# Turning the heads' outputs: TensorE transposes and one store against VectorE block transposes and stores in 128-byte pieces

## The chip, the cores and the metric

The kernel runs on one core of a Trainium2 chip. The metric is the time of one execution in device microseconds (us); the figure of a kernel is the median of its runs. Five engines work side by side, each with a queue of its own that is served strictly in order: TensorE (PE in the rows: matrix products and 128x128 transposes; PEld is its loading of weights), VectorE (DVE), ScalarE (ACT), GpSimd (POOL) and SyncE (SP), which only issues transfers (DMA). ACT and POOL issue transfers too. Engines wait for one another on semaphores.

## The reference

One decoder block over 512 rows (SEQ) of width 1024. One projection of the normalised input gives everything; the change lies in the mLSTM branch, four heads with outputs of 512 columns each:

```python
hn = rmsnorm(x, g_mix)
xa, ba, ca, za, q, k, v, o, zb, ig, fg, ga, gb = split(hn @ w_in)
ya = ((ba * causal_short_conv(ca * xa, conv_w, conv_b)) * silu(za)) @ w_a_out
hb = mlstm_chunkwise(q, k, v, ig + b_i, fg + b_f)          # 4 heads of 512 columns
hb = rmsnorm(hb, g_head)
yb = (sigmoid(o) * hb * silu(zb)) @ w_b_out
x  = x + (sigmoid(ga) * ya + sigmoid(gb) * yb) @ w_o
x  = x + sigmoid(rmsnorm(x, g_ple) @ w_ple_gate) * (p @ w_ple)
return rmsnorm(x, g_final)
```

`yb`'s product needs the heads' outputs with their columns on the partitions (the contraction runs over partitions), so what each head makes (rows on partitions) has to be turned.

## The kernel before

Every f32 product is made of three passes of fp32r products (`mm3`, L233 to L235) of a high part and a low part: ACT rounds an operand to its high part (`whi`, L180), DVE subtracts (`wlo`, L181). Weights come in chunks of 1 MB (`wraw`, four buffers) that SP loads (L148); POOL adds other chunks to them by accumulating transfers (L156), since most products run as one level of Strassen's scheme (`strassen`): seven products with about four chunks. Each product is two steps, each half of an operand is split once per step (`split_half`), and the weights' split buffers are two deep.

The order of the work is written out by hand: after each step of matmuls `step` calls `tick`, which advances every generator in `active` by one `yield`. A line of a generator between two yields thus stands in each engine's queue right behind the matmuls of that step. The order on PE, ACT, DVE and POOL is exactly the program's; SP's transfers are placed by a scheduler, and issued in its order.

Heads run one after the other. `head(h)` makes scores, the products for V and O, the weighted sum, and the gate; `y` (512 rows by 512 columns) is normed by `norm(t)` for its four row tiles t: in even heads inside a strassen run for the z gate (`sink_z`), in odd heads at once. Then `finish(h, y, wait)` waits some ticks and calls `turn`: 16 PE transposes in two groups of eight (tile `pty`), four ACT copies out of PSUM that also scale by `g_head` (`gh`, L805), and one POOL store of 1 MB into `yt_d[h]` (L813). Behind an even head runs a strassen for the merge gates (`sink_gate`), whose results `c` go through ACT's sigmoid and an ACT-issued store into `sg_d` (L782); the tag `c` has three buffers. `recut` loads the next head's q and k (`qk_d`) at that time. Behind head 3 the convolution begins (`sink_conv`), and its result tile `ya` uses the buffers of the tags `qk` and `vv`; the tile `yc` that holds the turned outputs has the tag `vv` too, of which there is one buffer.

Much later (about 628 us) POOL loads `yf[h]` from `yt_d[h]` (L1031), and `left_first` begins to make left operands of them (`left_high`, L1044 and L1045).

Of the kernel before, what the change touches and what calls it, by code (L numbers as in the profile page):

```python
# [9 lines left out]
F32 = mybir.dt.float32  # L10
F32R = mybir.dt.float32r
AF = mybir.ActivationFunctionType
ALU = mybir.AluOpType

P = 128
S = 512
NT = S // P
# [5 lines left out]
DV = 512  # L23
# [6 lines left out]
HC = 4  # L30
# [6 lines left out]
def hybrid_block(ctx, tc, x, p, g_mix, w_in, conv_w, conv_b, w_a_out, b_gates, g_head,  # L37
                 w_b_out, w_o, g_ple, w_ple_gate, w_ple, g_final, out):
    nc = tc.nc
    act, dve, pool, pe = nc.scalar, nc.vector, nc.gpsimd, nc.tensor  # L40
# [7 lines left out]
    ps_x = ctx.enter_context(tc.tile_pool(name="ps_x", bufs=4, space=bass.MemoryType.PSUM))  # L48
# [21 lines left out]
    H2 = S // 2  # L70
# [47 lines left out]
    spare = {b12[0]: None}  # L118
# [22 lines left out]
    raws, splits, pieces, active, fresh = {}, {}, deque(), [], []  # L141
# [111 lines left out]
    ident = const.tile([P, P], F32, name="ident")  # L253
# [14 lines left out]
    yt_d = [dram.tile([P, 2, HC, H2], F32, name=f"yt_d{h}") for h in range(NH)]  # L268
# [14 lines left out]
    def temp(tag, name=None, dt=F32):  # L283

        return tp.tile([P, S], dt, name=name or tag, tag=tag, bufs={"c": 3}.get(tag, 2))
# [238 lines left out]
    gh = prm[:, 40:56]  # L524
# [48 lines left out]
    def quarter(q):  # L573
        hi, lo = (u[:, q % HH, :] for u in splits[0][q // HH])
        return hi, lo, raws[0][:, q, :]
# [6 lines left out]
    hi, lo, raw = quarter(0)  # L582
# [118 lines left out]
    B = nc.vector.STREAM_SQUARE_SIZE  # L701
    rows32 = sp.tile([B, 8, S], F32, name="rows", tag="xin")
    rows = rows32[:NH]
# [92 lines left out]
        a = POFF[j] + (t - j) * P  # L796
        return u[:, a:a + P]

    def turn(h, y):

        yc = hp.tile([P, 2, 2, HC, H2], F32, name="yc", tag="vv", align_bytes=256)[:, 0]
        pts = {}
        for i in range(3):
            for v in range(2 * i - 2, 2 * i) if i else ():
                act.activation(yc[:, :, v, :], pts[v].rearrange("p (h s) -> p h s", h=2), AF.Copy,  # L805
                               scale=gh[:, 4 * h + v:4 * h + v + 1])
            for v in range(2 * i, 2 * i + 2) if i < 2 else ():
                pts[v] = ps_x.tile([P, S], F32, name="pty", tag="x")
                for t in range(NT):
                    pe.transpose(pts[v][:, t * P:(t + 1) * P], y[:, t, v * P:(v + 1) * P], ident)  # L810
            if i < 2:
                yield
        nc.gpsimd.dma_start(yt_d[h], yc)  # L813

    def qk_tile():
        both = hp.tile([P, 2, 4, S], F32R, name="qk", tag="qk", align_bytes=256)
        return [both[:, i] for i in range(2)]

    def recut(h, qk):

        for _ in range(7):
            yield
        raw = hp.tile([P, 2, 4, S], F32, name="qk_raw", tag="vv", align_bytes=256)[:, 0]
        for m in range(4):
            nc.sync.dma_start(raw[:, m, :], qk_d[h][:, m, :])
        yield
        yield
        yield
        qk.extend(qk_tile())
        for m in range(4):  # L830
            cut(qk[0][:, m, :], qk[1][:, m, :], raw[:, m, :])
            if m < 3:
                yield
# [69 lines left out]
    def head(h, qk):  # L903
        vv = []

        def sink_qk(n, t, src):

            fs, ps = slice(2 * (t % 2), 2 * (t % 2) + 2), slice(t // 2 * H2, (t // 2 + 1) * H2)
            src = src.rearrange("p (f s) -> p f s", f=2)
            if n == 1:  # L910
                nc.gpsimd.dma_start(qk_d[h + 1][:, fs, ps], src)
                return
            if not qk:
                qk.extend(qk_tile())
            cut(*[u[:, fs, ps] for u in qk], src)
            yield

        if h == 2:
            strassen(hn_lhs, sink_qk, True)
        pr = [hq2.tile([P, 1280], F32R, name=f"pr{i}", align_bytes=256) for i in range(2)]  # L920
        pp = hq2.tile([P, 1280], F32, name="pp")
        gt = []

        def sink_vo(n, t, src):
            if n == 0:
                if not vv:
                    both = hp.tile([P, 2, NT, DV], F32R, name="vv", tag="vv", align_bytes=256)
                    vv.extend(both[:, i] for i in range(2))
                act.activation(vv[0][:, t, :], src, AF.Copy)
                if t < 2:  # L930
                    yield
                dve.tensor_tensor(vv[1][:, t, :], src, vv[0][:, t, :].bitcast(F32), ALU.subtract)
            elif h % 2:
                so = temp("e", "so")
                act.activation(so, src, AF.Sigmoid)
                dve.tensor_tensor(gt[0][:, t, :], gt[0][:, t, :], so, ALU.mult)
            else:
                act.activation(gt[0][:, t, :], src, AF.Sigmoid)
            yield

        def scored():
            both = hp.tile([P, 2, NT, DV], F32, name="gty", tag="qk", align_bytes=256)
            gt.extend(both[:, i] for i in range(2))
            if h % 2:
                nc.gpsimd.dma_start(gt[0], z_d[h])

        active.append(scores(h, qk, pr, pp, scored))
        strassen(hn_lhs, sink_vo)
        gt, y = gt

        def weighted_sum(t, ps):
            dve.tensor_scalar(y[:, t, :], ps, inv[:, t:t + 1], None, ALU.mult)
            junk = temp("e", "junk")
            act.activation(junk, y[:, t, :], AF.Square, accum_out=hss[:, t:t + 1])
            yield

        for t in range(NT):
            ps = ps_x.tile([P, S], F32, name="pv", tag="x")
            for j in range(t + 1):
                mm3(ps, [ptile(u, j, t) for u in pr], [u[:, j, :] for u in vv], j == 0, j == t)  # L960
            step(weighted_sum(t, ps))

        def norm(t):
            dve.scalar_tensor_tensor(y[:, t, :], y[:, t, :], hr[:, t:t + 1], gt[:, t, :], ALU.mult, ALU.mult)

        def rsqrt():
            a, r, e = htmp
            dve.tensor_scalar(a, hss, 1.0 / DV, EPS, ALU.mult, ALU.add)
            pool.tensor_tensor(r, a, mhalf, ALU.pow)
            yield  # L970
            newton(e, a, r)
            dve.tensor_tensor(hr, r, e, ALU.mult)
            for t in range(NT) if h % 2 else ():
                norm(t)
                if t == 1:
                    yield

        def sink_z(n, t, src):
            sz = temp("e", "sz")
            act.activation(sz, src, AF.Sigmoid)  # L980
            if n == 1:
                dve.tensor_tensor(src, sz, src, ALU.mult)
                nc.gpsimd.dma_start(z_d[h + 1][:, t, :], src)
                yield
                return
            dve.tensor_tensor(sz, sz, src, ALU.mult)
            dve.tensor_tensor(gt[:, t, :], gt[:, t, :], sz, ALU.mult)
            yield
            norm(t)
            yield  # L990

        active.append(rsqrt())
        if h % 2 == 0:
            strassen(hn_lhs, sink_z)
        return y

    def finish(h, y, wait):
        for _ in range(wait):
            yield
        yield from turn(h, y)  # L1000

    hp_ctx, hp = open_pool("heads")
    hq_ctx, hq2 = open_pool("scores")
    load_maxima(0)
    qks = [qk_tile()] + [[] for _ in range(3)]
    for h in range(NH):
        y = head(h, qks[h])
        active.append(finish(h, y, 2 + h % 2))
        if h % 2 == 0:
            active.append(recut(h + 1, qks[h + 1]))  # L1010
            strassen(hn_lhs, sink_gate(h))
    close(hq_ctx)

# [15 lines left out]
    yf = {h: (wbp if h == 3 else yfp).tile([P, 2, HC, H2], F32, name=f"yf{h}", tag=f"yf{h}", align_bytes=256) for h in (0, 2, 1, 3)}  # L1029
# [6 lines left out]
    def left_high(k):  # L1036
# [7 lines left out]
        act.activation(units[k][0], src, AF.Copy, scale=scale)  # L1044
        return lambda: dve.scalar_tensor_tensor(both[:, 1], src, scale, both[:, 0].bitcast(F32), ALU.mult, ALU.subtract)  # L1045

    def left_first():
        for _ in range(5):
            yield
        for k in range(3):  # L1050
            low = left_high(k)
            yield
            low()
            yield
        for g in range(2):
            (a11, a21), (a12, a22) = ([yf[2 * g + r][:, v] for v in range(2)] for r in range(2))
            dve.tensor_tensor(hsf[g], a22, a21, ALU.subtract)
            yield
            dve.tensor_tensor(a21, a11, a21, ALU.subtract)
            yield  # L1060
            dve.tensor_tensor(a11, hsf[g], a11, ALU.add)
            yield
            if g == 0:
                dve.tensor_tensor(a12, a11, a12, ALU.subtract)
                yield
# [337 lines left out]
    q = [slice(CW, CW + CW // 2), slice(CW + CW // 2, D)]  # L1403
# [50 lines left out]
```

## Time and profile before

| what | us |
| --- | --- |
| median of 3 runs (lowest, highest) | 845.53 (845.3, 846.86) |
| the profiled execution | 847.37 |
| its span, as the trace has it | 845.6 |
| PE busy | 834.5 |
| DVE, ACT, POOL busy | 651.0, 495.5, 210.0 |
| granted TensorE clock, mean | 0.998 |

In the timelines a row is: start in us from the span's start, duration, engine, line, operation, out<-in tiles, shape, count, and in brackets how long the engine was idle before it and what ended that. `PEld` rows are weight loads. Rows with a q (SPq, ACTq) are the issue of a transfer.

### The profile page before, as it was taken

The page shows a single profiled execution, that of the slowest core. Times are in us where ns is not written, and L with a number is a line of the kernel's source. Part 1 is how long each engine was busy: PE and PEld are TensorE (multiplying, and loading weights), DVE is VectorE, ACT ScalarE, POOL GpSimd, SP SyncE. Part 2 cuts the span into 40 slices and gives each one's busy share as a digit, 9 for nine tenths or more (in the row PEclk, how much of TensorE's full clock was granted, in tenths as well). Part 3 has the DMA queues.
Part 4 walks back from the last instruction along what each step waited for, and adds up shares of the span by engine and source line. Part 5 has one row for each costly group of instructions (what it writes and reads, how often), then busy time and mean ns, then how long its engine had stood idle before and what let it go on. Part 6 is the DMA issues. An engine that isn't in the chain of part 4 may idle for free.

```text
span 845.6 us, 12113 instructions
## 1 busy us (share of the span) xinstructions
PE 834.5 (99%) x4584; PEld 726.7 (86%) x4584; DVE 651.0 (77%) x878; ACT 495.5 (59%) x720; POOL 210.0 (25%) x203
## 2 busy tenths in 40 slices
PE   8999999999999999999999999999999999999996
PEld 7888888887889988888788999999998888888885
DVE  5788767975787677788668779897986677999565
ACT  6467665666865566665776654555453256667543
POOL 5203122203124321220222333433411122131031
PEclk9999999999999999999999999999999999999999
DMA  9748779779978997896898799899989488999402
GB/s 310 269 145 183 159 166 220 194 274 227 252 159 207 244 225 180 199 215 199 258 243 211 156 218 169 194 184 182 181 255 380 101 194 214 284 258 229 187 0 100
DMA packets 103939, 173.89 MB, mean 206 GB/s; under 512 B 5632, under 2 KB 46132, under 8 KB 102600
## 3 DMA queue, kind: packets, MB, share of 16 engines
q0 software_dynamic: 39488, 70.33, 44.6%
q1 hardware_dynamic: 59792, 94.64, 33.7%
q10 hardware_dynamic: 4600, 8.14, 3.1%
q8 instruction: 36, 0.59, 0.3%
q14 instruction: 23, 0.19, 0.1%
HBM read 156.30 MB, written 16.79 MB: 205 GB/s over the span
## 4 chain that ended last, share of the span: by engine, by line
PE 92%; DMA 3%; DVE 2%; issue 1%; ACT 1%; SPq 0%; POOL 0%; POOLq 0%; ACTq 0%; DVEq 0%
PE mm L234 28%; PE mm L235 28%; PE mm L233 28%; PE pv L233 1%; PE pv L235 1%; PE pv L234 1%; DMA wraw<-in_w_ple 1%; DMA wraw<-in_w_b_out 1%; PE pty L810 1%; DMA sg_d<-c 1%; PE sc L235 1%; PE sc L234 1%; PE sc L233 1%; DVE wlo L181 1%; PE ptk L1247 0%
## 5 line engine op out<-in xcount | busy, mean ns | idle before, releaser
L181 DVE TENSOR_TENSOR wlo<-wraw,whi 128x1024 fp32r<-128x1024 f32 x244 | 299.4, 1229 | 104.7 <-ACT whi L180 98.8
L180 ACT ACTIVATE whi<-wraw 128x1024 fp32r<-128x1024 f32 x246 | 257.1, 1054 | 103.8 <-PE mm L235 48.8
L156 POOL DMA_DIRECT2D wraw<-in_w_in x112 | 136.9, 1423 | 335.4 <-DVE wlo L181 207.7
L346 ACT ACTIVATE s<-mm 128x512 f32<-128x512 f32 x84 | 50.2, 597 | 100.2 <-PE mm L235 98.7
L233 PE MATMUL mm<-whi,hs 128*128 128x512 f32 x256 | 99.9, 390 | 0.0
L234 PE MATMUL mm<-wlo,hs 128*128 128x512 f32 x256 | 99.8, 390 | 0.0
L235 PE MATMUL mm<-whi,hs 128*128 128x512 f32 x256 | 99.7, 389 | 0.0
L233 PE MATMUL mm<-hn_hi,whi 128*128 128x256 f32 (+1 forms) x304 | 93.3, 307 | 0.0
L235 PE MATMUL mm<-hn_hi,wlo 128*128 128x256 f32 (+1 forms) x304 | 92.9, 306 | 0.0
L234 PE MATMUL mm<-hn_lo,whi 128*128 128x256 f32 (+1 forms) x304 | 92.8, 305 | 0.0
L233 PE MATMUL mm<-hs,whi 128*128 128x256 f32 x320 | 90.9, 284 | 0.0
L234 PE MATMUL mm<-hs,whi 128*128 128x256 f32 x320 | 90.5, 283 | 0.0
L235 PE MATMUL mm<-hs,wlo 128*128 128x256 f32 x320 | 90.5, 283 | 0.0
L234 PE MATMUL mm<-wlo,hn_hi 128*128 128x512 f32 x192 | 75.3, 392 | 0.4 <-DVE wlo L181 0.2
L233 PE MATMUL mm<-whi,hn_hi 128*128 128x512 f32 x192 | 74.9, 390 | 0.0
L235 PE MATMUL mm<-whi,hn_lo 128*128 128x512 f32 x192 | 74.8, 389 | 0.0
L234 PEld LDWEIGHTS mm<-hs,whi 128*128 128x128 f32 x320 | 61.4, 192 | 0.0
L233 PEld LDWEIGHTS mm<-hs,whi 128*128 128x128 f32 x320 | 61.4, 192 | 0.0
L235 PEld LDWEIGHTS mm<-hs,wlo 128*128 128x128 f32 x320 | 61.4, 192 | 0.0
L235 PEld LDWEIGHTS mm<-hn_hi,wlo 128*128 128x128 f32 x304 | 58.1, 191 | 2.5
L234 PEld LDWEIGHTS mm<-hn_lo,whi 128*128 128x128 f32 x304 | 58.1, 191 | 2.4
L233 PEld LDWEIGHTS mm<-hn_hi,whi 128*128 128x128 f32 x304 | 58.1, 191 | 2.4
(339 smaller groups left out, 1670.2 us busy)
## 6 DMA issues: line engine op xcount, KB each, us to landing
wraw<-in_w_in SPq DMA_DIRECT2D x32, 1024.0 KB, 6.1
wraw<-in_w_in POOLq DMA_DIRECT2D x52, 512.0 KB, 8.5
wraw<-in_w_in SPq DMA_DIRECT2D x48, 512.0 KB, 5.6
wraw<-in_w_in POOLq DMA_DIRECT2D x60, 256.0 KB, 5.7
wraw<-in_w_b_out SPq DMA_DIRECT2D x7, 1024.0 KB, 7.0
wraw<-in_w_b_out POOLq DMA_DIRECT2D x12, 512.0 KB, 7.0
wraw<-in_w_o SPq DMA_DIRECT2D x5, 1024.0 KB, 7.4
yt_d<-yc POOLq DMA_DIRECT2D x4, 1024.0 KB, 4.9
```

The lines of the kernel that those rows point to most:

```text
L156: nc.gpsimd.dma_start(raws[to][:, ks, cs], src[:, ks, :], accum_op=ALU.add)
L180: act.activation(hi, t, AF.Copy)
L181: (e_lo or dve).tensor_tensor(lo, t, hi.bitcast(F32), ALU.subtract)
L233: pe.matmul(ps, lhsT=a[0], rhs=b[0], start=first, stop=False, **kw)
L234: pe.matmul(ps, lhsT=a[0], rhs=b[1], start=False, stop=False, **kw)
L235: pe.matmul(ps, lhsT=a[1], rhs=b[0], start=False, stop=last, **kw)
L346: act.activation(to[i], src, AF.Copy, scale=scale)
L810: pe.transpose(pts[v][:, t * P:(t + 1) * P], y[:, t, v * P:(v + 1) * P], ident)
```

## The change

The 64 PE transposes, the 16 ACT copies behind them and the four 1 MB stores go. Instead DVE transposes each row tile of `y` (128x512) in blocks of 32x32 (one instruction a tile, `turn`), into the first half of a `vv` buffer. That leaves the blocks themselves in the wrong places; the store places them: `put(i, b)` issues four transfers on SP, each from 32 partitions with 8x32 contiguous pieces of 32 elements, that is 256 pieces of 128 bytes. A head has eight puts, 32 transfers. `recut` uses the second half of the same buffer (`spare`) instead of a tile of its own. In even heads tiles 0 and 1 are turned inside the z strassen and put during the first four ticks behind the head, tiles 2 and 3 are turned four ticks later and put over four ticks more. In odd heads the tiles are turned from the fifth tick on and put over four ticks behind that; the first two cuts of q and k of head 2 come four ticks later than before. The scaling by `g_head` is done by 16 ACT instructions on the loaded `yf` in `left_first` (`scale_head`), in a loop that is one tick longer.

```diff
@@ -796,31 +796,55 @@
         a = POFF[j] + (t - j) * P
         return u[:, a:a + P]
 
-    def turn(h, y):
-
-        yc = hp.tile([P, 2, 2, HC, H2], F32, name="yc", tag="vv", align_bytes=256)[:, 0]
-        pts = {}
-        for i in range(3):
-            for v in range(2 * i - 2, 2 * i) if i else ():
-                act.activation(yc[:, :, v, :], pts[v].rearrange("p (h s) -> p h s", h=2), AF.Copy,
-                               scale=gh[:, 4 * h + v:4 * h + v + 1])
-            for v in range(2 * i, 2 * i + 2) if i < 2 else ():
-                pts[v] = ps_x.tile([P, S], F32, name="pty", tag="x")
-                for t in range(NT):
-                    pe.transpose(pts[v][:, t * P:(t + 1) * P], y[:, t, v * P:(v + 1) * P], ident)
-            if i < 2:
-                yield
-        nc.gpsimd.dma_start(yt_d[h], yc)
+    def turning(h):
+
+        both = hp.tile([P, 2, NT, DV], F32, name="yc", tag="vv", align_bytes=256)
+        blocks, spare = (both[:, i] for i in range(2))
+        blocks = blocks.rearrange("p t v -> p (t v)").rearrange("p (i v t c) -> p i v t c", i=2, v=HC, c=P)
+        to = yt_d[h].rearrange("p i v (t b a) -> p i (v t) b a", b=P // B, a=B)
+
+        def turn(y, t):
+            dve.transpose(blocks[:, t // 2, :, t % 2, :], y[:, t, :])
+
+        def put(i, b):
+            rows = blocks[b * B:(b + 1) * B, i].rearrange("p v t (q a) -> p (v t) q a", a=B)
+            for q in range(P // B):
+                nc.sync.dma_start(to[q * B:(q + 1) * B, i, :, b, :], rows[:, :, q, :])
+
+        return turn, put, spare
+
+    def finish(h, y, tools):
+
+        turn, put, _ = tools or turning(h)
+        if h % 2:
+            for ts in ((),) * 4 + (((0,), (1,), (2,), (3,)) if h == 1 else ((0, 1), (), (2,), (3,))):
+                for t in ts:
+                    turn(y, t)
+                yield
+            for b in range(P // B):
+                for i in range(2):
+                    put(i, b)
+                yield
+            return
+        for i in range(2):
+            for b in range(P // B):
+                put(i, b)
+                yield
+            if i == 0:
+                for _ in range(4):
+                    yield
+                for t in (2, 3):
+                    turn(y, t)
+                    yield
 
     def qk_tile():
         both = hp.tile([P, 2, 4, S], F32R, name="qk", tag="qk", align_bytes=256)
         return [both[:, i] for i in range(2)]
 
-    def recut(h, qk):
+    def recut(h, raw, qk):
 
         for _ in range(7):
             yield
-        raw = hp.tile([P, 2, 4, S], F32, name="qk_raw", tag="vv", align_bytes=256)[:, 0]
         for m in range(4):
             nc.sync.dma_start(raw[:, m, :], qk_d[h][:, m, :])
         yield
@@ -910,6 +934,8 @@
             if n == 1:
                 nc.gpsimd.dma_start(qk_d[h + 1][:, fs, ps], src)
                 return
+            for _ in range(4 if t < 2 else 0):
+                yield
             if not qk:
                 qk.extend(qk_tile())
             cut(*[u[:, fs, ps] for u in qk], src)
@@ -988,26 +1014,28 @@
             yield
             norm(t)
             yield
-
+            if t < 2:
+                yield
+                if not tools:
+                    tools.extend(turning(h))
+                tools[0](y, t)
+                yield
+
+        tools = []
         active.append(rsqrt())
         if h % 2 == 0:
             strassen(hn_lhs, sink_z)
-        return y
-
-    def finish(h, y, wait):
-        for _ in range(wait):
-            yield
-        yield from turn(h, y)
+        return y, tools
 
     hp_ctx, hp = open_pool("heads")
     hq_ctx, hq2 = open_pool("scores")
     load_maxima(0)
     qks = [qk_tile()] + [[] for _ in range(3)]
     for h in range(NH):
-        y = head(h, qks[h])
-        active.append(finish(h, y, 2 + h % 2))
+        y, tools = head(h, qks[h])
+        active.append(finish(h, y, tools))
         if h % 2 == 0:
-            active.append(recut(h + 1, qks[h + 1]))
+            active.append(recut(h + 1, tools[2], qks[h + 1]))
             strassen(hn_lhs, sink_gate(h))
     close(hq_ctx)
 
@@ -1044,14 +1072,23 @@
         act.activation(units[k][0], src, AF.Copy, scale=scale)
         return lambda: dve.scalar_tensor_tensor(both[:, 1], src, scale, both[:, 0].bitcast(F32), ALU.mult, ALU.subtract)
 
+    def scale_head(h):
+        for v in range(HC):
+            act.activation(yf[h][:, :, v, :], yf[h][:, :, v, :], AF.Copy, scale=gh[:, HC * h + v:HC * h + v + 1])
+
     def left_first():
         for _ in range(5):
             yield
+        for h in (0, 2):
+            scale_head(h)
+            yield
         for k in range(3):
             low = left_high(k)
             yield
             low()
-            yield
+            if k:
+                scale_head(2 * k - 1)
+                yield
         for g in range(2):
             (a11, a21), (a12, a22) = ([yf[2 * g + r][:, v] for v in range(2)] for r in range(2))
             dve.tensor_tensor(hsf[g], a22, a21, ALU.subtract)
```

On SP, between the loads of weights around the end of head 0 (wrawN is the N-th chunk of weights, qk_d1 the stored q and k of head 1, yt_d0 the turned output of head 0), stood before:

```order
L148 DMA wraw14_1277<-in_w_in 128x4x512
L148 DMA wraw15_1357<-in_w_in 128x4x512
L148 DMA wraw16_1403<-in_w_in 128x4x512
L825 DMA qk_raw_1651<-qk_d1_94 128x512
L148 DMA wraw17_1609<-in_w_in 128x4x512
L825 DMA qk_raw_1651<-qk_d1_94 128x512 x3
L148 DMA wraw18_1649<-in_w_in 128x4x512
L148 DMA wraw19_1692<-in_w_in 128x4x512
L148 DMA wraw20_1739<-in_w_in 128x4x512
```

and now:

```order
L148 DMA wraw14_1277<-in_w_in 128x4x512
L812 DMA yt_d0_90<-yc_1321 32x8x32 x5
L148 DMA wraw15_1360<-in_w_in 128x4x512
L812 DMA yt_d0_90<-yc_1321 32x8x32 x3
L148 DMA wraw16_1406<-in_w_in 128x4x512
L812 DMA yt_d0_90<-yc_1321 32x8x32 x8
L148 DMA wraw17_1602<-in_w_in 128x4x512
L148 DMA wraw18_1642<-in_w_in 128x4x512
L148 DMA wraw19_1685<-in_w_in 128x4x512
L812 DMA yt_d0_90<-yc_1321 32x8x32 x4
L148 DMA wraw20_1737<-in_w_in 128x4x512
L812 DMA yt_d0_90<-yc_1321 32x8x32 x12
```

Sixteen of the 32 transfers stand ahead of chunk 17, four ahead of chunk 20 and twelve behind it; the loads of q and k have moved ahead of chunk 13.

On DVE the turns of head 0's tiles 2 and 3 (`STREAM_TRANSPOSE yc<-gty`, L807) stand one behind each of the two splits of the 24th operand (`wlo240`, `wlo241`), each ahead of a result `c` of the gate strassen.

The second place is ACT, in the gate strassen behind head 0, where it issues the stores of the results (L782; whi261 is the high half of the 26th operand, L240 a cut of the next head's q and k). The semaphores waited for stand in brackets; DMAHW0 to DMAHW7 are the eight that all transfers of SP and ACT share. Before:

```order
L781 ACTIVATE c_1733<-c_1733 128x512 [waits DVE_49]
L782 DMA sg_d1_97<-c_1733 128x512 [waits Activation_49]
L781 ACTIVATE sg_1782<-mm_1459 128x512 [waits PE_49]
L782 DMA sg_d0_96<-sg_1782 128x512 [waits Activation_49]
L180 ACTIVATE whi261_1785<-wraw17_1609 128x1024
L240 ACTIVATE qk_1714<-qk_raw_1651 128x512 [waits DMAHW7_49]
L781 ACTIVATE c_1759<-c_1759 128x512 [waits DMAHW2_49,DVE_49]
L782 DMA sg_d1_97<-c_1759 128x512 [waits Activation_49]
```

and now:

```order
L781 ACTIVATE c_1731<-c_1731 128x512 [waits DMAHW6_49,DVE_49]
L782 DMA sg_d1_97<-c_1731 128x512 [waits DMAHW1_49,Activation_49]
L781 ACTIVATE sg_1788<-mm_1462 128x512 [waits PE_49]
L782 DMA sg_d0_96<-sg_1788 128x512 [waits DMAHW4_49,Activation_49]
L180 ACTIVATE whi261_1791<-wraw17_1602 128x1024
L240 ACTIVATE qk_1712<-yc_1321 128x512
L781 ACTIVATE c_1761<-c_1761 128x512 [waits DMAHW2_49,DVE_49]
L782 DMA sg_d1_97<-c_1761 128x512 [waits DMAHW1_49,Activation_49]
```

The rows are the same ones; what is new is that each store's issue waits for the transfer that used its semaphore last (a put, a load of SP or an earlier store), with the ACT rows behind it.

The third place is DVE at the beginning of the convolution, behind head 3 (cv and m are its intermediate tiles, ya1 its first result in the buffer that held the turned outputs). It stands now:

```order
L181 TENSOR_TENSOR wlo760_4787<-wraw46_4445,whi760_4786 128x1024 [waits DMAHW5_49,DMAHW4_49,Activation_49]
L410 TENSOR_TENSOR ya1_4754<-cv_4235,ya0_4753 128x2x256 [waits DMAHW4_49,DMAHW5_49,DMAHW3_49,DMAHW6_49,DMAHW2_49,DMAHW7_49,DMAHW1_49,DMAHW0_49]
L447 TENSOR_TENSOR m_4230<-m_4230,cz_4756 128x512
L181 TENSOR_TENSOR wlo761_4820<-wraw46_4445,whi761_4819 128x1024 [waits Activation_49]
L399 TENSOR_SCALAR cv_4235<-cu_4234,prm_174 128x256 [waits DVE_49]
```

Before, the L410 row waited for one semaphore, that of POOL's one store of head 3. Now it waits for all eight, that is for the last of head 3's 32 puts, and the split wlo761 stands two rows behind it. On SP these puts stand 3 behind chunk 45, 9 behind chunk 46, 12 behind chunk 47 and 8 behind chunk 48.

## The prediction

> **What bounds the kernel now.** I read the page's engine shares first, then busy times by stretch, then the chain of waits. The page's busy times:
>
> ```profile
> PE 834.5 (99%) x4584; PEld 726.7 (86%) x4584; DVE 651.0 (77%) x878; ACT 495.5 (59%) x720; POOL 210.0 (25%) x203
> ```
>
> PE is busy for 834.5 of a span of 845.6 us. The stretches tell where it isn't:
>
> ```profile
> core 0: us, PE busy (x) PEld busy (x) DVE busy (x) ACT busy (x) POOL busy (x), PEclk, DMA share, GB/s
> 20.00:195.00 175.00, 175.00 (x798) 145.47 (x797) 135.78 (x179) 110.42 (x166) 33.02 (x31) 1.00 0.76 203
> 195.00:200.00 5.00, 4.92 (x21) 3.46 (x20) 4.09 (x5) 3.79 (x6) 2.43 (x3) 1.00 0.87 283
> 200.00:404.00 204.00, 204.00 (x1088) 176.66 (x1087) 150.70 (x203) 126.13 (x189) 52.95 (x50) 1.00 0.88 211
> 404.00:418.00 14.00, 13.67 (x60) 10.67 (x59) 9.65 (x12) 11.23 (x18) 1.57 (x2) 1.00 0.83 268
> 418.00:820.00 402.00, 401.80 (x2452) 361.14 (x2451) 325.90 (x420) 223.20 (x306) 107.40 (x95) 1.00 0.84 204
> ```
>
> From 20 to 820 us PE stands still for 0.6 us in all (0.08 behind head 0, 0.33 behind head 2, 0.20 later), at a granted clock of 1.00. All heads lie there, so PE's work is the time, and whatever makes PE wait is added to it whole. The two small holes, at 195 and 404 us, lie behind the even heads, where the change acts, and there the transfers are at 0.87 and 0.83 of their engines' time: that is where a loss would start.
>
> **What is removed.** The chain of waits holds the transposes as eight rows, two for each head, each of eight transposes; the first and the last:
>
> ```profile
> 164.90 0.87 PE pty L810 x8
> ...
> 480.24 0.87 PE pty L810 x8
> ```
>
> Eight times 0.87 is 7.0 us of PE on the chain: the gain. What they feed (ACT copies, a store of 1 MB) isn't on the chain.
>
> **DVE turns.** 16 instructions of 128x512. The trace has four of that operation, and these gaps of DVE, near the ends of heads:
>
> ```profile
> L891 DVE STREAM_TRANSPOSE pp<-pp 128x512 f32<-128x512 f32 x4 | 2.8, 706 | 0.0
> 143.80 0.69 DVE L350 TENSOR_TENSOR c<-s,mm 128x512 f32<-128x512 f32 x1 [1.88 <-ACT s L346]
> 183.67 0.69 DVE L350 TENSOR_TENSOR c<-s,mm 128x512 f32<-128x512 f32 x1 [1.20 <-ACT s L346]
> 263.19 0.69 DVE L241 TENSOR_TENSOR qk<-c,qk 128x512 fp32r<-128x512 f32 x1 [1.93 <-ACT qk L240]
> 481.85 1.23 DVE L181 TENSOR_TENSOR wlo<-wraw,whi 128x1024 fp32r<-128x1024 f32 x1 [1.97 <-ACT whi L180]
> ```
>
> At 706 ns that is 11.3 us of DVE in all, 0.71 at a time, one in each tick but at head 3. DVE stands idle for 1.2 to 1.97 us before the next result or split, so the turns cost nothing. If that cover were gone, each turn would hold up the next split by 0.71, at most 11.3 in all.
>
> **ACT.** 16 copies go and 16 scalings of 128x512 come, late:
>
> ```profile
> L805 ACT ACTIVATE yc<-pty,prm x16: 672/682/692, 166.5 to 482.3; 128x512 f32<-128x512 f32 x16
> 640.00:656.00 16.00, 16.00 (x73) 13.23 (x72) 11.14 (x12) 5.22 (x6) 0.00 (x0) 1.00 0.96 368
> ```
>
> By 682 ns they are 10.9 us, in a stretch where ACT is busy for 5.2 of 16 us and PE never waits. They just fit; if the loads of `yf` come a tick later, the first left operands do too. I take 0 (bounds 0 to 3, less than a tick of 3.5, which is the distance of two gate stores below).
>
> **SP.** 32 issues a head, each with an issue time as in these rows (three in 1.62, two in 0.92):
>
> ```profile
> 176.64 1.62 SPq L825 DMA_DIRECT2D qk_raw<-qk_d  x3
> 501.25 0.92 SPq L148 DMA_DIRECT2D wraw<-in_w_in  x2
> ```
>
> At 0.5 us a head's puts hold SP for 16 us, over 8 to 12 ticks, that is about 2 us in a tick of 3.5. Weight loads behind them in SP's queue start up to 4 us later (eight puts between two chunks). Four buffers keep those loads more than one use ahead, so I take 0, and let the price of a piece carry what the DMA engines lose.
>
> **A piece of 128 bytes.** No row before has one. The 16 DMA engines' time by packets (packets, MB, share), for the whole run and in two windows (500 to 580 and 186 to 204 us), is nearest:
>
> ```profile
> q1 hardware_dynamic: 59792, 94.64, 33.7%
> ...
> q1 hardware_dynamic: 8367, 8.31, 33.8%
> ...
> q1 hardware_dynamic: 1113, 2.20, 38.4%
> ```
>
> A packet took 76 ns at 1583 bytes (0.337 x 845.6 x 16 / 59792), 51.7 ns at 993 and 99.4 ns at 1977. A line through pairs of these comes to 10 to 16 ns at 128 bytes; I take p = 13 ns. Below lies 6 ns (128/993 of 51.7), above 52 ns, if small packets cost as much as the smallest mean seen. A put is 256 pieces, 16 for each engine.
>
> [...]
>
> **Gate stores behind the even heads.** Around the hole at 195 us:
>
> ```profile
> 194.93 0.69 DVE L350 TENSOR_TENSOR c<-s,v 128x512 f32<-128x512 f32 x1 [2.77 <-DMA sg_d<-c]
> 195.54 1.22 DVE L181 TENSOR_TENSOR wlo<-wraw,whi 128x1024 fp32r<-128x1024 f32 x1
> 196.81 0.19 PEld L234 LDWEIGHTS mm<-wlo,hn_hi 128*128 128x128 f32 x1 [0.40 <-DVE wlo L181]
> ...
> 194.35 0.33 ACTq L782 DMA_DIRECT2D sg_d<-c  x1
> 197.85 0.33 ACTq L782 DMA_DIRECT2D sg_d<-c  x1
> ...
> sg_d<-c ACTq DMA_DIRECT2D x4, 256.0 KB, 3.9
> ```
>
> DVE waits 2.77 us for a store of `c` to free its buffer, the split queued behind it follows, and PE waits 0.40 for the split: no slack. The store takes 3.9 us; in that time one tick's four puts share its engines, 64 pieces on each, 64p = 0.83. Twice (heads 0 and 2): 128p = 1.66 us. The new semaphore waits of ACT's issues: the store at 197.85 waits for the one of 194.35, which lands at 194.35 + 3.9 = 198.25, so 0.4 late, with a sigmoid and a weight rounding behind it on ACT, and DVE's split behind that. I take 0, as that split is a step ahead; bounds 0 and 2.
>
> **Weights behind them.** The twelve puts behind chunk 20 (three ticks, about 10 us) run beside the accumulating transfers that the next splits wait for (head 0, then head 2):
>
> ```profile
> 208.39 1.06 ACT L180 ACTIVATE whi<-wraw 128x1024 fp32r<-128x1024 f32 x1 [2.47 <-DMA wraw<-in_w_in]
> 209.48 1.23 DVE L181 TENSOR_TENSOR wlo<-wraw,whi 128x1024 fp32r<-128x1024 f32 x1 [1.71 <-ACT whi L180]
> 210.76 0.19 PEld L234 LDWEIGHTS mm<-wlo,hs 128*128 128x128 f32 x1
> ...
> 426.27 1.06 ACT L180 ACTIVATE whi<-wraw 128x1024 fp32r<-128x1024 f32 x1 [1.62 <-DMA wraw<-in_w_in]
> 427.36 1.23 DVE L181 TENSOR_TENSOR wlo<-wraw,whi 128x1024 fp32r<-128x1024 f32 x1 [0.86 <-ACT whi L180]
> 429.60 0.19 PEld L234 LDWEIGHTS mm<-wlo,hs 128*128 128x128 f32 x1
> ```
>
> ACT waits 2.47 us for the transfer; the split ends at 210.71 and PE uses it at 210.76. Half of the twelve puts fall into that transfer's time, 96p = 1.25 us late, all of it PE's. At head 2 the split ends at 428.59, 1.0 ahead of its use: 96p - 1.0 = 0.25. Together 1.5.
>
> **The convolution's first write.**
>
> ```profile
> 509.51 0.68 DVE L410 TENSOR_TENSOR ya<-cv,ya 128x512 fp32r<-128x512 f32 x1
> 511.58 1.23 DVE L181 TENSOR_TENSOR wlo<-wraw,whi 128x1024 fp32r<-128x1024 f32 x1 [0.78 <-ACT whi L180]
> 513.82 0.19 PEld L235 LDWEIGHTS mm<-hn_hi,wlo 128*128 128x128 f32 x1
> ...
> wraw<-in_w_in SPq DMA_DIRECT2D x16, 512.0 KB, 4.4
> ...
> yt_d<-yc POOLq DMA_DIRECT2D x4, 1024.0 KB, 4.9
> ```
>
> The store of 1 MB took 4.9 us and was long done here. Now L410 waits for the last of 32 puts, eight of them behind chunk 48, whose pair is issued from 501.25 and lands 4.4 later. Eight issues at 0.5, a put in flight and some waiting for semaphores bring it to about 511.5 (estimate from these rows), 2 us later than L410 stands now. Behind it on DVE stand `m` and the split of 511.58, whose end at 512.81 is 1.0 ahead of its use; with 0.78 idle ahead of it too, 2.0 late leaves nothing to 1.2; I take 0.8 (bounds 0 to 3).
>
> **Sum.** -7.0 + 1.66 + 1.25 + 0.25 + 0.8 = -3.04. The profiled execution's 847.37 would become 844.3. It stands 1.84 above the median of 845.53; on the median it is 842.5. In p the sum is 320p - 7.2.
>
> **Rivals.** *All hidden:* the puts run in the gaps of the transfers and nothing waits: 845.53 - 7.0 = 838.5. The share of 0.76 in the first stretch speaks for it, 0.87 behind head 0 against it. This stands for p of 6 ns or less as well (320p - 7.2 = -5.3, 840.2).
>
> *Given back whole:* p between 17 and 28 ns puts the sum between -1.7 and +1.7. [...] The same outcome has a second way: the transfers of weights are the bound behind the even heads, PE comes there 1.74 us earlier twice and only waits longer, so 3.5 of the gain goes and -3.0 becomes +0.5: 846.0. The wait of 2.47 us for a transfer speaks for it; against it, those transfers are started by work that PE paces, so that they come earlier too. [...]
>
> *Slower:* small pieces cost a fixed time each. From 22.5 ns on the change loses; at 28 ns it is +1.7, at 42 ns +6.2 (851.8), at 52 ns +9.4 (855). The place is the gate stores and the weights behind heads 0 and 2, with no slack in the rows above. Against it speaks the fall from 99 to 52 ns when a packet halves, which leaves little that is fixed.
>
> *The change doesn't do what it says:* the transposes go from PE in any case; only where PE would wait in their place is open, and that is the second way above.
>
> **How the numbers follow.** Less than 0.2%, 1.7 us, can't be told from no change. Chances: all hidden (838.5 to 840.2) 0.22; part given back (p of 6 to 17 ns, 840.2 to 843.8, its own range) 0.34; given back whole (843.8 to 847.2) 0.20; slower (847.2 to 855) 0.24. So faster 0.56, same 0.20, slower 0.24. The likeliest is the second case, with 842.5 from the sum. The range leaves out the upper part of the slower case, from p = 42 ns on, some 0.1, and little below all hidden: 838.3 to 852.
>
> **What the profile after would show.** Right: no `pty`, PE busy about 7 us less; 16 transposes on DVE of 0.7 us with no split waiting behind them; packets of q1 32,768 more, and their share grown by p of 13 ns each (0.4 ms over 16 engines, 3% of the span); holes of PE of 1 to 3 us only near 195 to 210, 404 to 430 and 511 to 515 us. Wrong: a share of q1 grown by more than 6% (p over 25 ns), or stores of `sg_d` of 6 us; PE waiting at ends of odd heads; SP late with weights; or PE holes at 640 to 660 behind the scalings.

## The result, and the profile after

The changed kernel takes 867.07 us (866.33 to 868.26, 4 runs) against 845.65: a ratio of 1.0252, 95% interval 1.0234 to 1.027. It is 21.4 us slower; the prediction was 842.5 with a range of 838.3 to 852. The page of the changed kernel, and the same stretches of time as before (its span is 865.3 us, so each lies up to 20 us earlier in the program):

```profile
PE 837.0 (97%) x4520; PEld 724.0 (84%) x4520; DVE 659.5 (76%) x894; ACT 495.3 (57%) x720; POOL 207.8 (24%) x199
...
core 0: us, PE busy (x) PEld busy (x) DVE busy (x) ACT busy (x) POOL busy (x), PEclk, DMA share, GB/s
20.00:195.00 175.00, 174.46 (x784) 143.90 (x782) 139.96 (x184) 108.23 (x162) 33.16 (x31) 1.00 0.77 201
195.00:200.00 5.00, 5.00 (x23) 3.86 (x22) 1.83 (x2) 2.01 (x3) 2.85 (x4) 1.00 1.13 275
200.00:404.00 204.00, 197.25 (x1015) 168.57 (x1014) 147.14 (x203) 119.87 (x179) 50.68 (x46) 0.97 0.89 201
404.00:418.00 14.00, 14.00 (x64) 11.59 (x63) 12.36 (x14) 7.83 (x12) 0.00 (x0) 1.00 0.77 243
418.00:820.00 402.00, 390.96 (x2380) 350.20 (x2379) 317.89 (x409) 226.24 (x310) 100.87 (x90) 0.99 0.87 210
```

PE has 64 instructions fewer and is yet busy for 2.5 us longer. Between 200 and 820 us it stands still for 17.8 us, where it was 0.5 before, and in two stretches the granted clock is below 1. What PE waits for:

```profile
PE mm L233 <- ACT v L346: 7.1, 2, 4.7
PE mm L235 <- DVE wlo L181: 6.0, 1, 6.0
PE mm L234 <- DVE wlo L181: 3.4, 6, 1.0
```

Two waits of ACT and one of DVE make 13.1 us. What those engines waited for stands in the view of the tile `yc` (the turned blocks): who waited for transfers of it, in us and times, and how long those took to land:

```profile
  ACT vv L955: 16.8, 3
  DVE ya L410: 7.7, 1
...
DMA to landing us min/median/max: 1.7/5.5/16.8
```

These are waits for puts (a put, from here on, is one of the transfers of 256 pieces). The view also puts 6.5 us of POOL down to a put, but in the kernel before POOL is idle for 6.49 us at the same place, so that is no loss. The timelines show the four large waits, three of them with PE's row behind the hole (the first held PE up by 0.1 us itself):

```profile
218.21 0.63 ACT L955 ACTIVATE vv<-c 128x512 fp32r<-128x512 f32 x1 [4.72 <-DMA yt_d<-yc]
...
313.04 0.63 ACT L955 ACTIVATE vv<-c 128x512 fp32r<-128x512 f32 x1 [6.77 <-DMA yt_d<-yc]
314.21 0.80 PE L233 MATMUL mm<-whi,hs 128*128 128x512 f32 x1 [4.66 <-ACT v L346]
...
446.09 0.63 ACT L955 ACTIVATE vv<-c 128x512 fp32r<-128x512 f32 x1 [5.27 <-DMA yt_d<-yc]
447.26 0.50 PE L233 MATMUL mm<-whi,hs 128*128 128x512 f32 x1 [2.44 <-ACT v L346]
...
529.32 0.69 DVE L410 TENSOR_TENSOR ya<-cv,ya 128x512 fp32r<-128x512 f32 x1 [7.70 <-DMA yt_d<-yc]
531.80 0.58 PE L235 MATMUL mm<-hn_hi,wlo 128*128 128x256 f32 x1 [6.03 <-DVE wlo L181]
```

`vv` is the next head's V. It lies in the one buffer of its tag, which the turned blocks held until the last put had landed. On SP, eight puts behind head 1 take 10.87 us to be issued, with a load of weights behind them:

```profile
290.60 10.87 SPq L812 DMA_DIRECT2D yt_d<-yc  x8
301.57 4.70 SPq L148 DMA_DIRECT2D wraw<-in_w_in  x1
```

Where the time goes, by the start of the same matrix product in the two traces (after minus before, in us):

| matmul at (before) | delay | what lies between |
| --- | --- | --- |
| 158.2 | +0.2 | head 0 up to its end |
| 169.1 | -1.4 | two groups of transposes gone |
| 204.8 | +2.3 | holes of 0.81 and 0.76, then a slow clock |
| 218.2 | +3.4 | weights late, and ACT's first wait for `vv` |
| 262.3 | +1.7 | two groups gone |
| 310.6 | +9.1 | the hole of 4.66, then a slow clock |
| 387.7 | +7.9 | two groups gone |
| 437.1 | +12.4 | small holes at 430, the hole of 2.44 |
| 454.2 | +13.6 | a hole of 0.99 behind POOL's load of `gty` |
| 480.9 | +12.1 | two groups gone |
| 515.3 | +19.7 | the hole of 6.03, then a slow clock |
| the end | +19.8 | |

### The profile page after: what moved, and what is told of

Its sections match the earlier page's. It is cut to its first block, busy times and chain, and to the rows that moved or that the text cites. A ratio compares the mean times of both kernels' runs of the same rounds, so it can differ in the third digit from the quotient of the medians.

```text
span 865.3 us, 12151 instructions
## 1 busy us (share of the span) xinstructions
PE 837.0 (97%) x4520; PEld 724.0 (84%) x4520; DVE 659.5 (76%) x894; ACT 495.3 (57%) x720; POOL 207.8 (24%) x199
## 4 chain that ended last, share of the span: by engine, by line
PE 75%; DMA 12%; DVE 5%; ACT 3%; SPq 3%; issue 2%; ACTq 0%; POOL 0%; POOLq 0%; DVEq 0%
PE mm L234 23%; PE mm L235 23%; PE mm L233 23%; DMA yt_d<-yc 7%; DMA wraw<-in_w_in 2%; SPq L812 2%; DVE wlo L181 2%; ACT whi L180 1%; PE pv L235 1%; PE pv L234 1%; PE pv L233 1%; DMA wraw<-in_w_b_out 1%; DMA xin<-in_x 1%; DMA z_d<-c 0%; PE ptk L1284 0%
## 5 line engine op out<-in xcount | busy, mean ns | idle before, releaser
L156 POOL DMA_DIRECT2D wraw<-in_w_in x112 | 137.1, 1448 | 387.7 <-DVE wlo L181 204.4
L233 PE MATMUL mm<-whi,hs 128*128 128x512 f32 x256 | 101.3, 396 | 7.5 <-ACT v L346 7.1
L235 PE MATMUL mm<-whi,hs 128*128 128x512 f32 x256 | 100.7, 393 | 0.0
L233 PEld LDWEIGHTS mm<-whi,hs 128*128 128x128 f32 x256 | 48.6, 190 | 18.9 <-ACT v L346 7.8
```

Source lines behind the costliest of these rows:

```text
L156: nc.gpsimd.dma_start(raws[to][:, ks, cs], src[:, ks, :], accum_op=ALU.add)
L233: pe.matmul(ps, lhsT=a[0], rhs=b[0], start=first, stop=False, **kw)
L235: pe.matmul(ps, lhsT=a[1], rhs=b[0], start=False, stop=last, **kw)
```

## The experiments

The kernel before took 846.0 to 846.3 us beside these runs.

**One store in place of the puts.**

```diff
 def put(i, b):
-    rows = ...
-    for q in range(P // B):
-        nc.sync.dma_start(...)
+    if i == 1 and b == P // B - 1:
+        nc.gpsimd.dma_start(yt_d[h], <the blocks as they lie>)
```

> Leaves out the placing: the turned blocks of a head go to DRAM as they lie, by one POOL store of 1 MB where the last put stood (the blocks stay in the wrong places). The turns on DVE and the late scaling on ACT stay. Three theories of the loss. Turns: the DMA engines take packets of different queues in turn, so each of a put's 16 small packets on an engine waits for a 2048-byte packet of POOL's accumulating transfers (median 176 ns), 2.9 us a put, and the late puts hold buffers that ACT and DVE wait for. Price: the 128-byte pieces take engine time (15 ns, 31 us over 16 engines) and weights come late for it. Issue: 128 more issues on SP and the eight shared semaphores hold up SP's weight loads. All three: 838.5, within 838 to 840, PE without new holes. If it stays over 845, the turns on DVE or the scaling cost what was thrown on the puts.

846.81 us, ratio 1.0002 (0.9991 to 1.0013). All three theories missed: the large holes are gone, but the gain isn't kept. The start of products stood 3.8 us ahead of before at head 2's end (417 to 441 us) and 0.9 behind it at 454 us, by three holes of 0.68 to 0.76 us and 3.4 us at half the clock (mean granted clock 0.995, before 0.998). The store stands in the burst of accumulating transfers behind the even heads; behind head 0 the chain of waits runs through these:

```profile
196.79 8.35 DMA wraw<-in_w_in
207.85 13.95 DMA wraw<-in_w_in
```

The second one, the same transfer as the one issued at 211.01 in the kernel before, took 10.54 there. So 1 MB in that burst costs time in one plain store too.

**The same transfers in pieces of 1 KB.**

```diff
-    rows = blocks[b * B:(b + 1) * B, i].rearrange("p v t (q a) -> p (v t) q a", a=B)
+    rows = blocks[b * B:(b + 1) * B, i].rearrange("p v t c -> p v (t c)")
     for q in range(P // B):
-        nc.sync.dma_start(to[q * B:(q + 1) * B, i, :, b, :], rows[:, :, q, :])
+        nc.sync.dma_start(yt_d[h][b * B:(b + 1) * B, i, q], rows[:, q])
```

> The same 128 SP transfers in the same places with the same bytes, each in 32 pieces of 1 KB in place of 256 of 128 bytes (so the blocks land in wrong places). Turns: two packets an engine and put, some 0.4 us beside accumulating transfers; the holes at 309, 445 and 526 us go, 838.5 to 843. Price: 46 ns for 1 KB, 11.8 us of engine time in place of 31, so about 0.38 of the loss of 28 us stays: 849. Issue: the number of issues and semaphores is the same, so nothing changes: 864 to 868.

850.86 us, ratio 1.0043 (1.0026 to 1.006): 16.2 of the 21.4 us go with the number of pieces alone, at the same bytes, issues and places. That refutes the theory of issues as the main cause, but the time lies nearest to what the theory of price gave (849), not to the theory of turns (838.5 to 843), so this run doesn't tell those two apart. PE no longer waits for `vv`, and behind `ya` for 0.3 us only; the longest hole that is left, 2.15 us, stands behind this:

```profile
203.50 0.33 ACTq L782 DMA_DIRECT2D sg_d<-sg  x1
203.87 1.06 ACT L180 ACTIVATE whi<-wraw 128x1024 fp32r<-128x1024 f32 x1 [1.74 <-DMA yt_d<-yc]
```

ACT's issue of a gate store waits for a put with the same semaphore, and the rounding of weights behind it is late: this part is what the theory of issues says. The other holes, 6.8 us in all between 150 and 730 us, were not traced to a cause.

**Puts issued by POOL.**

```diff
-                nc.sync.dma_start(to[q * B:(q + 1) * B, i, :, b, :], rows[:, :, q, :])
+                nc.gpsimd.dma_start(to[q * B:(q + 1) * B, i, :, b, :], rows[:, :, q, :])
```

> The same 128-byte pieces, issued by POOL in the same places. Turns: the puts stand in the same queue as the accumulating transfers and no longer share the engines with them packet by packet, each takes 0.2 to 0.5 us when its turn comes, but POOL needs 0.6 to 1.2 us for each issue, which delays accumulating transfers: 842 to 852. Price: the pieces cost the same: 862 to 868. Issue: SP is free of the puts: 840 to 848, with SP's weight loads as before the change.

861.55 us, ratio 1.0164 (1.0138 to 1.019): near the theory of price, but not for its reason. Within a group the puts land 0.2 to 0.6 us apart (in the median 3.9 us from issue to landing, 5.5 in the changed kernel), SP is free of them (which by the theory of issues gave 840 to 848), and the holes have moved: 4.69 us at 285, where DVE waits 8.84 for a store of `qk_d` that stands behind 24 puts in POOL's queue, and 4.65 at 514, where `ya` still waits for the last put:

```profile
287.66 0.69 DVE L350 TENSOR_TENSOR c<-s,v 128x512 f32<-128x512 f32 x1 [8.84 <-DMA qk_d<-c]
...
516.19 0.69 DVE L410 TENSOR_TENSOR ya<-cv,ya 128x512 fp32r<-128x512 f32 x1 [6.31 <-DMA yt_d<-yc]
```

**Other buffers, puts on SP as in the changed kernel.** The second half of a head's blocks gets a buffer of its own, head 3's lie in the tile `m`, and in odd heads the first half's puts go ahead of the second's.

```diff
-        both = hp.tile([P, 2, NT, DV], F32, name="yc", tag="vv", align_bytes=256)
+        if h < 3:
+            both = hp.tile([P, 2, NT, DV], F32, name="yc", tag="vv", align_bytes=256)
+            halves = [<the first 4 KB of both>, hp.tile([P, 2 * DV], F32, name="yd", tag="yd", align_bytes=256)]
+        else:
+            halves = [m[:, i] for i in range(2)]
...
-            for b in range(P // B):
-                for i in range(2):
-                    put(i, b)
+            for k in range(0, 8, 2):
+                for n in (k, k + 1):
+                    put(n // 4, n % 4)
```

> Output as in the reference. The second half of a head's turned blocks gets a buffer of its own (4 KB), so that only the first half's puts hold the buffer that the next head's vv needs; head 3's blocks lie in the unused half of the merge tile m, so that the convolution's ya does not wait for puts. In odd heads the first half's eight put groups come ahead of the second's. Turns: puts stay slow (2.6 us apart beside accumulating transfers), but PE's holes of 4.66, 2.44 and 6.03 us and the slower clock behind them (2.6 and 1.5 us) go: 847 to 853. Price: weights stay late, only the wait for the buffers goes: 855 to 864. Issue: SP's queue is as long as before: 858 to 866.

847.05 us, ratio 1.0008 (0.9986 to 1.003), the low end of what the theory of turns gave, and 8 us below the theory of price. The puts are as slow as in the changed kernel (2.6 to 3.1 us apart behind head 0) and cost the same engine time; q1 in the changed kernel, then here:

```profile
q1 hardware_dynamic: 94608, 98.85, 36.8%
...
q1 hardware_dynamic: 94608, 98.85, 38.0%
```

Yet 20 us are gone, of the 28.4 that lie between the changed kernel and the gain that was due. So the theory of price is out, and most of the loss was the wait for two buffers, with what followed from it. (Some 1.6 of the 20 are luck: the holes of 1.14 and 0.75 us behind head 0 bring no half clock here, with a mean granted clock of 0.997, see below.) What is left is a load on SP that lands 16 us after its issue beside puts, and a gate store that takes 6.5 us, for which the next gate store's issue waits, as the chain of waits shows at 290 and 193 us:

```profile
290.60 16.07 DMA wraw<-in_w_in
...
193.60 6.50 DMA sg_d<-c
```

**The removal alone.**

```diff
-        yc = hp.tile(...)
-        <16 transposes, four copies>
-        nc.gpsimd.dma_start(yt_d[h], yc)
+        yield
+        yield
+        nc.gpsimd.dma_start(yt_d[h].rearrange("p i v s -> p (i v s)"), y.rearrange("p t s -> p (t s)"))
```

> The kernel before without the 64 PE transposes and the 16 ACT copies; POOL's 1 MB store stands at the same place and stores the heads' outputs unturned and unscaled. It tells what the removal is worth by itself. If PE's 7.0 us come out whole: 838.5, within 838 to 840. If the weights' transfers behind heads 0 and 2 are the bound there, PE only waits longer: 3.5 us of it stay, 842.

848.82 us, ratio 1.0027 (1.0016 to 1.0038): slower, against both forecasts, by a wait that the edit itself made. The store now reads `y`, and behind head 1 ACT waits for it to free the buffer of the tag `qk`:

```profile
266.16 0.63 ACT L240 ACTIVATE qk<-c 128x512 fp32r<-128x512 f32 x1 [10.06 <-DMA yt_d<-gty]
```

PE stands still for 5.73 us there. Everywhere else the products come earlier by 0.8 to 0.9 us behind each group that is gone, and keep it through the bursts. The wait and the half clock behind it (mean granted clock 0.993) cost 7.9 us by the products' starts, and the last product is 0.6 late, so without them it would be some 7.2 early (an estimate). The removal is worth what was forecast, and a transfer that holds a buffer can take it back.

**Plain stores in quiet places.** The buffers of the run before last, but each half goes out in one POOL store of 512 KB, in even heads the second one behind the burst.

```diff
+            if b == q == 0:
+                nc.gpsimd.dma_start(yt_d[h][:, i].rearrange("p v s -> p (v s)"), halves[i].rearrange("p v t c -> p (v t c)"))
```

> The turns on DVE, the late scaling and the buffers of the run named buffers, but each head's turned blocks go out as they lie, in two POOL stores of 512 KB, the second behind the gate products' accumulating transfers in even heads. It leaves out the placing. If turns and scaling are hidden and the loss of the run with one store came from where that store stood (in the burst of accumulating transfers behind heads 0 and 2), this is as fast as the removal by itself: 838 to 841. If the turns on DVE delay splits: 844 to 848, with PE waiting for DVE behind the turns.

841.72 us, ratio 0.9941 (0.9921 to 0.996). Its page:

```profile
PE 827.4 (99%) x4520; PEld 720.3 (86%) x4520; DVE 660.8 (79%) x894; ACT 495.6 (59%) x720; POOL 212.1 (25%) x207
```

In the profiled executions PE is busy for 7.1 us less than before and the last product comes 6.5 earlier; by the medians the gain is 4.3, with four runs. No hole stands behind the turns on DVE or the late scaling.

**Puts on POOL, in quiet places, with the new buffers.**

```diff
-                nc.sync.dma_start(...)
+                nc.gpsimd.dma_start(...)
+        yield from puts(0, 4)          # even heads: first half, four transfers a tick
+        ...                            # turn the second half, then eight ticks behind the burst
+        yield from puts(1, 2)
+            yield from puts(0, 4 if h == 1 else 1)
+            for _ in range(6 if h == 1 else 0):
+                yield
+            yield from puts(1, 2 if h == 1 else 1)
```

> Output as in the reference. The 128-byte puts are issued by POOL, so that they stand in line with the accumulating transfers and not against them; the buffers are those of the run named buffers; the first half of a head is put four transfers a tick where POOL has no accumulating transfers, the second half two a tick (head 3 one a tick) behind the burst. Turns: no put is in an engine's queue beside a burst, no buffer is waited for, ACT's stores share no semaphore with a put: 838.5 to 842. Price: the pieces still take 31 us of engine time, weights late as in the changed kernel: 855 to 865. Issue: 128 issues of 0.58 us on POOL delay accumulating transfers: 844 to 850.

845.77 us, ratio 1.0003 (0.9977 to 1.003), scattered from 840.28 upwards: unclear by itself. Its one large hole is 4.17 us at 233, behind this row:

```profile
234.82 0.69 DVE L976 TENSOR_TENSOR gty<-gty,so 128x512 f32<-128x512 f32 x1 [5.25 <-DMA gty<-z_d]
```

The load of `gty` stands behind ten puts and two accumulating transfers on POOL.

**The same, with that load ahead of the puts.**

```diff
-        for _ in range(8):
+        for _ in range(13):
             yield
-        yield from puts(1, 2)
+        yield from puts(1, 4)
-            for _ in range(6 if h == 1 else 0):
+            for _ in range(10 if h == 1 else 0):
```

> Output as in the reference. As the run named poolbuf, with the second half's puts moved behind POOL's load of gty (even heads, four a tick) and behind the last accumulating transfer of the first gate products (head 1), since in poolbuf DVE waited 5.25 us for that load behind four puts. Turns: no hole at 233 us; 840 to 842, the time of the run named halves (841.7), clear of the kernel before. Price: the pieces' engine time stays, so no better than poolbuf, 845 to 850. Issue: POOL's 128 issues delay the accumulating transfers of the next products: 845 to 850, with holes at 245 to 270 us.

841.37 us, ratio 0.9941 (0.992 to 0.9962): faster than both kernels, with the same placing in pieces of 128 bytes as the changed kernel, and level with the plain stores. Its page and packets, then the packets of the changed kernel:

```profile
PE 828.3 (99%) x4520; PEld 720.0 (86%) x4520; DVE 660.0 (78%) x894; ACT 496.1 (59%) x720; POOL 282.8 (34%) x327
...
DMA packets 107459, 173.89 MB, mean 207 GB/s; under 512 B 7616, under 2 KB 48116, under 8 KB 106632
q0 software_dynamic: 43008, 70.34, 45.6%
...
DMA packets 138180, 173.89 MB, mean 201 GB/s; under 512 B 40385, under 2 KB 80885, under 8 KB 137353
q0 software_dynamic: 38912, 66.14, 41.7%
```

POOL's 128 issues (75 us more of its time than in the changed kernel) are hidden. But the small packets are gone as well. Issued by SP, each piece of 128 bytes is a packet of its own, 32,768 in all. Issued by POOL, the 4.2 MB of puts that q0 has more than in the changed kernel are 2048 packets of 2 KB (the other 2048 packets that it has more are under 512 B): 16 for each put, one for 16 of its 256 pieces. So POOL's queue packed the pieces here, in the first run with puts on POOL too (q0 there: 43008 packets, 70.34 MB as well), and these runs say nothing on what single pieces cost. No run separates the packing from the other ticks.

## Why the prediction was wrong, by its steps

**The gain of 7.0 us, the turns and the scaling** were right. The products' starts move by 0.9 us at nearly every group, and these rows have no wait behind them; their instructions took

```profile
L807 DVE STREAM_TRANSPOSE yc<-gty 128x512 f32<-128x512 f32 x16 | 11.1, 700 | 0.0
L1077 ACT ACTIVATE yf<-yf,prm 128x512 f32<-128x512 f32 x16 | 10.1, 708 | 0.0
```

against 706 and 682 ns in the sum.

**The price of a piece**, 13 ns, was right as engine time where little else ran, with some luck: two of the three pairs of points in the prediction give 10 and 16 ns, the third, of 1583 and 1977 bytes, gives less than nothing. In the whole run q1 has 34,816 packets more and, by its share, 15.4 ns for each (0.368 x 865.3 less 0.337 x 845.6, times 16). Between 286 and 290 us, where almost nothing else ran, it is 12.2 ns (0.315 x 4.0 x 16 / 1652), and in the burst, from 204 to 210 us, 25.7 ns (0.112 x 6.0 x 16 / 418). The two windows:

```profile
q1 hardware_dynamic: 1652, 0.20, 31.5%
q0 software_dynamic: 37, 0.08, 21.5%
...
q0 software_dynamic: 459, 0.89, 80.2%
...
q1 hardware_dynamic: 418, 0.05, 11.2%
```

**The step that failed first is "64p = 0.83"**: a put's delay was taken to be the sum of its pieces' own times. In the burst q0 (POOL's accumulating transfers, 1.9 KB a packet) and q1 (the puts) had almost the same number of packets served, 459 and 418, but 0.89 and 0.05 MB. The counts fit engines that turn from one queue to the other packet for packet, so that each of the 16 pieces that an engine has of a put (256 over 16 engines) waits for a packet of 168 ns (0.802 x 6.0 x 16 / 459). By this estimate a put takes 2.7 us, where 0.2 was counted, and four puts in a row behind head 0 landed 2.6 to 2.7 us apart (208.27, 210.88, 213.56, 216.17). The run with 1 KB pieces, two packets on each engine, took 16 us of the loss away. What a packet is depended on the queue in these runs, one piece of 128 bytes where SP issued the puts and 16 pieces, 2 KB, where POOL did; the two counts, nearly level, are of such packets.

**The step that was left out is the buffer.** The sum has a term for `ya` (0.8, bounds 0 to 3; measured 6.03) and none for `vv`, the other user of the same buffer: 16.8 us of ACT's waits, 7.1 us of PE's. Before, each 1 MB store, which took 4.9 us, had landed 31 to 39 us before the next `vv` was written, so that no row showed a wait. Late puts became late buffers, and late buffers PE's holes; the run with other buffers shows it.

**The gate stores and ACT's shared semaphores.** The sum lets a gate store behind each even head be 0.83 late, and puts at 0 (bounds 0 to 2) the wait of the next store's issue for it. Behind head 0 the store of 193.50 landed 6.15 us after its issue (before: 3.99, the store of 194.35). The issue of 199.73 waits for the same semaphore (DMAHW1 in the listing of ACT ahead of the prediction) and came only then; ACT stood still for 2.7 us, the rounding of 201.14 was late, and PE's holes of 0.81 and 0.76 follow it:

```profile
193.50 0.33 ACTq L782 DMA_DIRECT2D sg_d<-c  x1
...
196.39 0.62 ACT L781 ACTIVATE c<-c 128x512 f32<-128x512 f32 x1
199.73 0.33 ACTq L782 DMA_DIRECT2D sg_d<-c  x1
...
201.14 1.06 ACT L180 ACTIVATE whi<-wraw 128x1024 fp32r<-128x1024 f32 x1 [0.44 <-DMA yt_d<-yc]
```

Only the 0.44 is put down to a put; in the run with 1 KB pieces such an issue waits for a put itself. By the products' starts PE lost 1.8 us here without the clock and 1.2 behind head 2, so 3.0 where 1.66 was counted. The weights (1.25 and 0.25) cost up to 1.0, between 205 and 218 us, where ACT's first wait for `vv` ends too. The 1.3 at 454 us has no term: it follows POOL's load of `gty`, which took 9.05 us to land (7.93 before). All this is 5.3 against 3.2: too small, but not what decided.

**The slow clock** was in no step. In these rows of 3.41 us each, the granted clock, third figure from the end, comes out as 1.00 or 0.50:

```profile
200.58:203.99 3.41, 1.84 (x7) 1.00 (x6) 1.56 (x2) 2.97 (x5) 0.65 (x1) 1.00 1.21 210
203.99:207.40 3.41, 3.41 (x10) 2.62 (x9) 2.12 (x2) 1.92 (x3) 0.78 (x1) 0.50 1.11 250
...
309.81:313.22 3.41, 0.00 (x0) 0.00 (x0) 0.00 (x0) 0.18 (x1) 0.00 (x0) 1.00 1.10 327
313.22:316.63 3.41, 2.42 (x6) 1.96 (x7) 1.50 (x2) 3.41 (x8) 0.00 (x0) 0.50 0.15 57
...
442.92:446.33 3.41, 1.90 (x12) 1.49 (x10) 0.00 (x0) 0.24 (x1) 0.00 (x0) 1.00 1.09 275
446.34:449.75 3.41, 2.17 (x8) 1.52 (x9) 1.56 (x2) 3.41 (x8) 0.00 (x0) 1.00 0.20 72
449.76:453.17 3.41, 3.41 (x19) 2.91 (x19) 2.65 (x5) 3.10 (x6) 0.41 (x1) 1.00 0.77 229
...
524.85:528.25 3.40, 0.92 (x8) 0.71 (x6) 0.00 (x0) 1.59 (x2) 0.00 (x0) 1.00 1.38 199
528.26:531.67 3.41, 0.00 (x0) 0.00 (x0) 2.35 (x4) 1.06 (x1) 0.00 (x0) 0.50 0.01 1
```

It fell at 203.99, 313.22 and 528.26, for 3.41, 6.83 and 6.83 us, and the three starts are 32 and 63 slots of 3.413 us apart. The rows fit a decision slot by slot, on PE's work in the slot before: the two short holes ahead of 203.99 lie in one slot, which leaves 1.84 us of work in it, and the next slot runs at half clock; the other two falls stand behind slots with 0.00 and 0.92 us of work. The hole of 2.44 is cut by such a border at 446.34 (71 slots behind 203.99), which leaves 1.90 and 2.17 us of work on its two sides, and the clock stays at 1.00. Between 1.84 and 1.90 lies little, so what exactly is counted stays open.

By the delays of the products the three cost 1.6, 2.6 and 1.5 us. Two holes cost 0.27 us more than their length until products follow at their old distance (one of 0.76 puts the next products back by 1.03, one of 0.99 by 1.26); taking this for all 14 holes over 0.1 us is an estimate. The account: holes +17.3, clock +5.7, 14 holes of 0.27 +3.8, transposes -7.1, in all +19.7 of the 19.8 that the last product is late.

**The rivals.** "Slower" came, but not by its mechanism: it asked for pieces of 28 ns or more, and they cost 15.4 in the mean and 12.2 where little else ran; the 25.7 ns of the burst came beside other packets. Put into the prediction's sum, even 25.7 gives a loss of 1.0 us (320p - 7.2), not of 21.4. "PE only waits longer for weights" is refuted by the plain stores in quiet places, whose last product keeps 6.5 of the 7.0 us.

## What to carry to other kernels

Cost a store in small pieces not by its bytes or by the engine time of its pieces, but by the number of packets times the packet time of whatever queue it runs beside (here 16 x 168 ns, 2.7 us for a put); then move it away from bursts, or into a queue that packs the pieces (POOL's did here, 16 to a packet), and read the packets in the trace before pricing them. Ask of every transfer that becomes slower which buffer it holds and who writes that buffer next, even where the trace of before shows no wait for it, because there it was merely early. The same placing from another queue, at other ticks and in another buffer turned 2.5% of loss into 0.6% of gain.

## What the runs showed of the hardware that was not expected

A hole of PE can cost more than its length: behind the holes of 4.66 and 6.03 us, and behind two of 0.81 and 0.76, the granted clock was 0.50 for one or two slots of 3.41 us, while behind the one of 2.44 it stayed at 1.00. In the changed kernel's trace, away from its ends, the three slots at full clock ahead of a fall held 1.84, 0.00 and 0.92 us of PE's work, and every other slot at full clock 1.90 us or more. The run with other buffers has holes of 1.14 and 0.75 us behind head 0 as well, and its mean granted clock was 0.997 (0.987 in the changed kernel): no half clock followed; where the slots' borders lay there is not shown. In the changed kernel a slot that was half busy (1.84 of 3.41) was enough for a fall.

Small pieces were packets of their own in SP's queue and were packed, 16 to a packet of 2 KB, in POOL's. And POOL's 128 issues of a put of 256 pieces took 75 us of its time, 0.59 us each (282.8 less 207.8, over 128), and could be hidden on an engine that is busy for a third of the time.
